# Seven products instead of eight in the first MLP product, and one token part after the other

## The chip, the cores and the metric

The kernel runs on one core of one Trainium2 chip. The metric is device time of one execution, in microseconds, as the median of several runs.

## The reference, cut to what matters

Two blocks follow each other. The first has two layers of mixing (attention and two convolution branches) and an MLP; its layer 0 runs over 512 latent and 256 context tokens, its layer 1 over the 512 latent ones. The second block has two hybrid layers and is not touched. The model width is 1024, the MLP's inner width 4096. What the change bears on, for each layer of the first block:

```python
def sqrelu_mlp(h, w1, w2):
    a = jax.nn.relu(h @ w1)          # h: T x 1024, w1: 1024 x 4096
    return (a * a) @ w2              # w2: 4096 x 1024

h2 = modulate(rmsnorm(xl_new, g_pre_mlp[i]), ml[3], ml[4])
xl_new = xl_new + ml[5] * rmsnorm(sqrelu_mlp(h2, w_mlp_in[i], w_mlp_out[i]), g_post_mlp[i])
```

T is 768 in layer 0 (both kinds of tokens go through the same weights) and 512 in layer 1. Everything is in float32.

## The kernel before, in words

A float32 product is made of three matmuls: every operand is split into a high part (a cast on ScalarE, ACT, line L336) and a low part (a subtraction on VectorE, DVE, L337), and low x high, high x low and high x high are summed in PSUM on TensorE (PE). `mm3` (L368 to L370) does that for one pair of operands; `fm` (L372, its matmul on L383) does it for 128 weight columns over all eight chunks of 128 of the inner dimension. Where there are two token parts (512 and 256 columns in layer 0), `fm` goes through both with each weight part, so that matmuls of 512 and 256 columns alternate.

The MLP (`mlp`, from L1163) works in eight groups of four blocks of 128 columns of W1. For each block: `fm` over T tokens into PSUM, then `square` (relu L1175 and square L1178 on ACT, square and low part L1179 and L1180 on DVE). Then the W2 product of the group for all T/128 token tiles, 512 output columns at a time: 24 matmuls of 512 a tile and group, so 144 in layer 0 and 96 in layer 1, added to the sums in SBUF by DVE (L1220; in group 0 copied by ACT, L1218). The first group is begun while the mixing ends: `early` makes its first two blocks in two parts, and the transposes of the normalized tiles (`prenorm`, L465, with the normalization L460 before and the splits L495 and L496 behind) stand between these parts. Weights come in loads of 512 KB on SyncE's (SP's) queue (L353) into SBUF blocks `at_16_f`, whose places a packer (`pack`) plans ahead; a load's start is set by what freed its place.

The program is written by generators (`yield` gives way to the next stage's work, with a cost in us); a scheduler then sets the order on each engine by the times it expects, and every engine runs its queue in that order. `conv_proj` in layer 0's mixing uses `fm` too, over 512 and 256 columns. In layer 0's MLP the modulation products of layer 1 (L602) and its first columns are woven in.

## Time and profile before

| | us |
| --- | --- |
| median of 3 runs (2879.17 to 2883.06) | 2882.73 |
| the profiled execution's own time | 2879.93 |
| its span | 2878.2 |
| PE busy / DVE busy / ACT busy | 2755.5 / 1623.9 / 1113.5 |

The span runs from the first instruction to the last. An engine is busy while an instruction of it runs; matmuls overlap each other, so that a busy PE says that matmuls follow without a break and not how fast. The time from one matmul's start to the next one's is its pitch. MLP groups run from about 434 to 972 us in layer 0 and from 1281 to 1630 in layer 1.

### The profile page before, as it was taken

The page shows a single profiled execution, that of the slowest core. Times are in us where ns is not written, and L with a number is a line of the kernel's source. Part 1 is how long each engine was busy: PE and PEld are TensorE (multiplying, and loading weights), DVE is VectorE, ACT ScalarE, POOL GpSimd, SP SyncE. Part 2 cuts the span into 40 slices and gives each one's busy share as a digit, 9 for nine tenths or more (in the row PEclk, how much of TensorE's full clock was granted, in tenths as well). Part 3 has the DMA queues.
Part 4 walks back from the last instruction along what each step waited for, and adds up shares of the span by engine and source line. Part 5 has one row for each costly group of instructions (what it writes and reads, how often), then busy time and mean ns, then how long its engine had stood idle before and what let it go on. Part 6 is the DMA issues. An engine that isn't in the chain of part 4 may idle for free. (4 is left out here: it accounts for less than half of the span.)

```text
span 2878.2 us, 37990 instructions
## 1 busy us (share of the span) xinstructions
PE 2755.5 (96%) x14735; PEld 2278.5 (79%) x14735; DVE 1623.9 (56%) x2767; ACT 1113.5 (39%) x2180; POOL 477.6 (17%) x680
## 2 busy tenths in 40 slices
PE   6999999999999899989999899999899999998999
PEld 4877678888888776678888777789788877888887
DVE  4786652434334786653444679655543679565632
ACT  5337643222222526643323444333432543333431
POOL 2024220000000213210000001323221012333111
PEclk9999999999999999999999999999999999999999
DMA  6233444312222333543322422232342522232232
GB/s 225 71 94 112 123 148 145 97 59 63 68 64 68 120 103 96 184 141 108 110 81 80 132 63 69 56 97 62 83 117 75 143 54 57 71 93 63 80 107 81
DMA packets 333564, 277.93 MB, mean 97 GB/s; under 512 B 30340, under 2 KB 275016, under 8 KB 333384
## 3 DMA queue, kind: packets, MB, share of 16 engines
q1 hardware_dynamic: 332410, 273.28, 32.2%
q8 instruction: 116, 1.90, 0.3%
q0 software_dynamic: 704, 2.13, 0.2%
q14 instruction: 64, 0.52, 0.1%
q10 hardware_dynamic: 270, 0.09, 0.0%
HBM read 258.65 MB, written 14.45 MB: 95 GB/s over the span
## 5 line engine op out<-in xcount | busy, mean ns | idle before, releaser
L383 PE MATMUL bank<-at_r,at_r 128*128 128x512 f32 (+1 forms) x5568 | 1214.8, 374 | 2.4 <-ACT at_r L495 2.2
L383 PEld LDWEIGHTS bank<-at_r,at_r 128*128 128x128 f32 x5568 | 965.7, 190 | 187.4 <-issue 8.0
L337 DVE TENSOR_TENSOR at_r<-at_f,at_r 128x1024 fp32r<-128x1024 f32 (+6 forms) x448 | 494.1, 1113 | 486.3 <-ACT at_r L336 380.7
L368 PE MATMUL bank<-at_r,at_r 128*128 128x512 f32 (+5 forms) x1832 | 673.5, 368 | 27.5 <-ACT at_r L336 10.8
L369 PE MATMUL bank<-at_r,at_r 128*128 128x512 f32 (+5 forms) x1832 | 659.6, 360 | 1.8 <-DVE at_r L337 1.8
L370 PE MATMUL bank<-at_r,at_r 128*128 128x512 f32 (+5 forms) x1832 | 658.9, 360 | 0.0
L336 ACT CAST at_r<-at_f 128x1024 fp32r<-128x1024 f32 (+4 forms) x450 | 412.9, 929 | 622.4 <-PE bank L370 190.7
L368 PEld LDWEIGHTS bank<-at_r,at_r 128*128 128x128 f32 x1832 | 350.6, 192 | 104.9 <-issue 16.9
L369 PEld LDWEIGHTS bank<-at_r,at_r 128*128 128x128 f32 x1832 | 351.7, 192 | 49.8 <-DVE at_r L337 4.5
L370 PEld LDWEIGHTS bank<-at_r,at_r 128*128 128x128 f32 x1832 | 350.9, 192 | 48.1 <-issue 1.2
L449 POOL MEMSET at_f<- 128x1 f32 x34 | 3.4, 106 | 888.5 <-DMA at_f<-in_w_q_b_dram 504.6
L1175 ACT ACTIVATE at_f<-bank 128x768 f32<-128x768 f32 (+1 forms) x64 | 45.1, 705 | 258.7 <-PE bank L383 258.7
L516 POOL TENSOR_SCALAR at_f<-at_f,mx 128x768 f32<-128x768 f32 (+3 forms) x112 | 95.3, 853 | 239.8 <-DVE mx L515 221.7
L1220 DVE TENSOR_TENSOR at_f<-at_f,bank 128x512 f32<-128x512 f32 x120 | 81.0, 685 | 54.2 <-PE bank L370 54.0
L1179 DVE TENSOR_TENSOR at_f<-at_f 128x768 f32<-128x768 f32 (+1 forms) x64 | 52.6, 822 | 101.4 <-ACT at_r L1178 101.4
L513 DVE TENSOR_REDUCE mx<-bank 128x1 f32<-128x768 f32 (+1 forms) x80 | 67.6, 845 | 25.7 <-PE bank L370 25.5
L1994 POOL TENSOR_TENSOR at_f<-at_f 128x512 f32<-128x512 f32 x32 | 50.4, 1575 | 178.7 <-DVE at_f L1993 156.5
L336 ACT CAST at_r<-bank 128x256 fp32r<-128x256 f32 (+4 forms) x124 | 51.5, 425 | 68.6 <-PE bank L1943 33.4
L337 DVE TENSOR_TENSOR at_r<-bank,at_r 128x256 fp32r<-128x256 f32 (+4 forms) x124 | 58.9, 483 | 29.7 <-ACT at_r L336 28.7
L514 ACT ACTIVATE at_f<-bank,mx 128x768 f32<-128x768 f32 (+1 forms) x80 | 65.6, 821 | 21.6 <-DVE mx L513 19.0
L1002 PE MATMUL bank<-ident,at_f 128*128 128x128 f32 x416 | 63.0, 279 | 5.6 <-ACT at_f L1006 2.9
L602 PE MATMUL bank<-at_f,at_f 128*32 128x512 f32 x384 | 60.7, 619 | 5.3 <-DMA at_f<-in_w_mod_dram 5.3
(294 smaller groups left out, 2922.7 us busy)
## 6 DMA issues: line engine op xcount, KB each, us to landing
at_f<-in_w_in_dram SPq DMA_DIRECT2D x148, 512.0 KB
at_f<-in_w_mod_dram SPq DMA_DIRECT2D x96, 512.0 KB
at_f<-in_w_mlp_in_dram SPq DMA_DIRECT2D x64, 512.0 KB
at_f<-in_w_mlp_out_dram SPq DMA_DIRECT2D x64, 512.0 KB
at_f<-d SPq DMA_DIRECT2D x28, 512.0 KB
at_f<-in_w_branch_dram SPq DMA_DIRECT2D x48, 256.0 KB
d<-at_f SPq DMA_DIRECT2D x22, 512.0 KB
at_f<-in_w_o_dram SPq DMA_DIRECT2D x16, 512.0 KB
```

What stands on the lines that cost most here:

```text
L336: self.nc.scalar.copy(hi, src)
L337: (self.nc.gpsimd if pool else self.nc.vector).tensor_tensor(lo, src, hi.bitcast(F32), op=OP.subtract)
L368: mm(ps, L[1], R[0], start=start, stop=False)
L369: mm(ps, L[0], R[1], start=False, stop=False)
L370: mm(ps, L[0], R[0], start=False, stop=stop)
L383: mm(ps[:, o:o + b - a], w[x][:, k], hl[y][:, k, a:b], start=k == 0 and j == 0, stop=k == nk - 1 and j == 2)
L513: nc.vector.tensor_reduce(mx[:, 0:1], ps, axis=AX, op=OP.max, negate=True)
L514: nc.scalar.activation(P, ps, AF.Exp, bias=mx[:, 0:1], accum_out=mx[:, 1:2])
L516: nc.gpsimd.tensor_scalar(P, P, mx[:, 2:3], 1.0, op0=OP.mult, op1=OP.mult)
L602: nc.tensor.matmul(ps[q:q + 32], self.sT[:, k], raws[j - 1 + k // 2 % 2][:, k % 2], start=k < 4, stop=k >= 4)
L1002: nc.tensor.transpose(pt[:, k], P[:, k * 128:(k + 1) * 128], self.ident)
L1220: nc.vector.tensor_tensor(y, y, ps[t], op=OP.add)
```

## The change

In groups 1 to 7 of both layers, two blocks of 128 columns of W1 are made together. Tokens, inner dimension and weight columns are each cut in halves, and the 2 x 2 by 2 x 2 product of quarters is made from seven products (`seven`, 84 matmuls of T/2 columns) instead of eight. `wsums` loads 256 columns of W1 (1 MB), makes four sums of weight quarters on DVE and splits all seven weight operands. `hsums` makes four sums of activation quarters once a layer, within the W2 product of group 0: the normalized rows are written to DRAM by `prenorm` (`keep`) and read back, because only their split parts stay in SBUF. Each product is evicted from PSUM by adds on DVE (L1267, one copy on ACT) that combine it with others; relu then works in place in SBUF. `fm` now goes through one token part after the other, and in layer 0 the parts of the MLP's first group are 384 and 384. The packer's constants change too.

```diff
-SPARES, TRIES = (16.0, 8.0, 4.0, 2.0, 1.0, 0.0), 30
+SPARES, TRIES = (4.0, 2.0, 1.0, 0.0), 60
 FLOOR = 60.0
-KEY = lambda B: lambda i: (-min(int((B[i, 4] - B[i, 3]) / 100), 3), -B[i, 0], B[i, 1] - B[i, 2])
+KEY = lambda B: lambda i: B[i, 3] - B[i, 4]
...
     def fm(self, ps, w, parts, nk=8):
         mm = self.nc.tensor.matmul
-        todo, o = [], 0
+        o = 0
         for hl, a, b in parts:
-            todo.append((hl, a, b, o))
+            for k in range(nk):
+                h, q = (hl, k) if len(hl) == 2 else (hl[k // 4 * 2:k // 4 * 2 + 2], k % 4)
+                for j, (x, y) in enumerate(((1, 0), (0, 1), (0, 0))):
+                    mm(ps[:, o:o + b - a], w[x][:, k], h[y][:, q, a:b], start=k == 0 and j == 0,
+                       stop=k == nk - 1 and j == 2)
+                yield 3 * (b - a) / 2400.0
             o += b - a
-        n = sum(b - a for _, a, b, _ in todo)
-        for k in range(nk):
-            for j, (x, y) in enumerate(((1, 0), (0, 1), (0, 0))):
-                for hl, a, b, o in todo:
-                    mm(ps[:, o:o + b - a], w[x][:, k], hl[y][:, k, a:b], start=k == 0 and j == 0,
-                       stop=k == nk - 1 and j == 2)
-            yield 3 * n / 2400.0
...
+            if keep is not None:
+                nc.sync.dma_start(keep.rearrange("p (k f) -> p k f", k=8), y)
...
-        L["h2"], L["h2c"] = self.HL(8, 512), None
+        n = T // 256
+        L["h2"], L["h2c"] = self.HL(8, 128 * n if n > 2 else 512), None
+        L["rows"] = self.dram([T, 1024])
...
+                if T > 512:
+                    L["h2c"] = self.HL(4, 128 * n) + self.HL(4, 128 * n)
...
+    def hsums(self, L):
...
+        B = L["B"] = {x: self.HL(4, 128 * n) for x in names}
+        def one(t):
+            s = slice(t * 128, t * 128 + 128)
+            part = lambda x, src: self.split(src, *(z[:, :, s] for z in B[x]))
+            o, y, d = self.A(8, 128), self.A(8, 128), self.A(2, 4, 128)
+            for z, r in ((o, t), (y, t + n)):
+                nc.sync.dma_start(z, L["rows"][r * 128:(r + 1) * 128].rearrange("p (k f) -> p k f", k=8))
+            sub = lambda z, a, b: nc.vector.tensor_tensor(z, a, b, op=OP.subtract)
+            sub(d[:, 0], y[:, 0:4], o[:, 0:4])
+            sub(d[:, 1], y[:, 4:8], d[:, 0])
+            part("T1", d[:, 0])
+            part("T2", d[:, 1])
+            sub(y[:, 0:4], y[:, 4:8], y[:, 0:4])
+            part("T3", y[:, 0:4])
+            sub(o[:, 4:8], o[:, 4:8], d[:, 1])
+            part("T4", o[:, 4:8])
+            self.F(o, y, d)
...
+    def wsums(self, W, c0):
+        nc = self.nc
+        r = self.raw(8, 256)
+        nc.sync.dma_start(r, W[:, c0:c0 + 256].rearrange("(k p) n -> p k n", p=128))
+        a11, a12, a21, a22 = (r[:, k:k + 4, x:x + 128] for x in (0, 128) for k in (0, 4))
+        s = self.A(2, 4, 128, lead=self.PART)
+        HL = lambda *n: [self.A(*n, dt=F32R, lead=self.PART) for _ in range(2)]
+        tt = nc.vector.tensor_tensor
+        wa, wb, ws = HL(8, 128), HL(4, 128), [HL(2, 4, 128) for _ in range(2)]
+        self.split(r[:, :, 0:128], *wa)
+        tt(s[:, 0], a21, a22, op=OP.add)
+        tt(s[:, 1], s[:, 0], a11, op=OP.subtract)
+        self.split(s, *ws[0])
+        tt(s[:, 0], a11, a21, op=OP.subtract)
+        tt(s[:, 1], a12, s[:, 1], op=OP.subtract)
+        self.split(s, *ws[1])
+        self.split(a22, *wb)
+        self.F(r, s)
...
+    def seven(self, ps, w, h):
+        mm = self.nc.tensor.matmul
+        for k in range(4):
+            for j, (x, y) in enumerate(((1, 0), (0, 1), (0, 0))):
+                mm(ps, w[x][:, k], h[y][:, k], start=k == 0 and j == 0, stop=k == 3 and j == 2)
+            yield 3 * ps.shape[1] / 2400.0
...
+        half, quick = T // 2, True
+        if quick and T > 512:
+            early = later = [(h2, 0, half), (h2c, 0, half)]
...
+        def pair(c0):
+            add = lambda o, a, b: nc.vector.tensor_tensor(o, a, b, op=OP.add)
+            w, held = self.wsums(W1, c0)
+            B, x = L["B"], [self.A(T) for _ in range(2)]
+            u, y = self.A(half), [r[:, i * half:(i + 1) * half] for r in x for i in range(2)]
+            def product(i, j, *sums):
+                ps = self.P(half)
+                yield from self.seven(ps, w[i], B[j])
+                if not sums:
+                    nc.scalar.copy(u, ps)
+                for o, z in sums:
+                    add(o, z, ps)
+                self.F(ps)
+            yield from product("11", "11")
+            yield from product("12", "21", (y[0], u))
+            yield from product("S2", "T2", (u, u))
+            yield from product("S1", "T1", (y[1], u))
+            yield from product("S3", "T3", (y[3], y[1]), (u, u))
+            yield from product("S4", "22", (y[1], y[1]))
+            yield from product("22", "T4", (y[2], u))
+            self.F(u, held)
+            nc.scalar.activation(x[0], x[0], AF.Relu)
+            nc.scalar.activation(x[1], x[1], AF.Relu)
+            for r in x:
+                hi, lo = self.HL(T)
+                nc.scalar.activation(hi, r, AF.Square)
+                nc.vector.tensor_tensor(r, r, r, op=OP.mult)
+                nc.vector.tensor_tensor(lo, r, hi.bitcast(F32), op=OP.subtract)
+                self.F(r)
+                aT.append((hi, lo))
...
+            if quick and g:
+                for p in range(2):
+                    yield from pair((4 * g + 2 * p) * 128)
...
-                ps = self.P(T)
-                yield from self.fm(ps, w, later)
+                ps = self.P(2, 512) if wide else self.P(T)
+                if wide:
+                    for i in range(2):
+                        yield from self.fm(ps[:, i, :half], w, later[i:i + 1])
+                else:
+                    yield from self.fm(ps, w, later)
...
+            if quick and g == 0:
+                sums = self.hsums(L)
...
+                        if sums:
+                            sums.pop(0)()
```

Three places of the new order. On PE, the start of a steady layer-0 group (W2 product of one group, then W1 product of the next), before:

```order
L370 MATMUL bank<-at_16_r,at_12_r 128x512
L383 MATMUL bank<-at_64_r,at_16_r 128x512
L383 MATMUL bank<-at_32_r,at_16_r 128x256
L383 MATMUL bank<-at_64_r,at_16_r 128x512
L383 MATMUL bank<-at_32_r,at_16_r 128x256
L383 MATMUL bank<-at_64_r,at_16_r 128x512
```

and now, the whole W1 product of the group (two pairs of 84):

```order
L370 MATMUL bank<-at_16_r,at_12_r 128x512
L1233 MATMUL bank<-at_24_r,at_16_r 128x384 x17
L1233 MATMUL bank<-at_48_r,at_16_r 128x384 x24
L1233 MATMUL bank<-at_24_r,at_16_r 128x384 x31
L1233 MATMUL bank<-at_24_r,at_8_r 128x384 x12
L1233 MATMUL bank<-at_48_r,at_16_r 128x384 x24
L1233 MATMUL bank<-at_24_r,at_16_r 128x384 x48
L1233 MATMUL bank<-at_24_r,at_8_r 128x384 x12
```

Alternating matmuls of 512 and 256 columns, each with its own weights, have become runs of 384 columns. On DVE, in a steady layer-0 group, before (the adds of the W2 product L1220, the splits of the next weights L337, the squares of a block):

```order
L1220 TENSOR_TENSOR at_16_f<-at_16_f,bank 128x512 x6
L337 TENSOR_TENSOR at_16_r<-at_16_f,at_16_r 128x1024
L1220 TENSOR_TENSOR at_16_f<-at_16_f,bank 128x512 x6
L337 TENSOR_TENSOR at_16_r<-at_16_f,at_16_r 128x1024 x3
L1179 TENSOR_TENSOR at_12_f<-at_12_f 128x768
L1180 TENSOR_TENSOR at_12_r<-at_12_f,at_12_r 128x768
L337 TENSOR_TENSOR at_16_r<-at_16_f,at_16_r 128x1024
L1179 TENSOR_TENSOR at_12_f<-at_12_f 128x768
L1180 TENSOR_TENSOR at_12_r<-at_12_f,at_12_r 128x768
L337 TENSOR_TENSOR at_16_r<-at_16_f,at_16_r 128x1024 x2
L1179 TENSOR_TENSOR at_12_f<-at_12_f 128x768
L1180 TENSOR_TENSOR at_12_r<-at_12_f,at_12_r 128x768
```

and now, from the last adds of the W2 product (L1347) through the weight sums (L1215 to L1219) and splits into the first adds out of PSUM (L1267):

```order
L1347 TENSOR_TENSOR at_16_f<-at_16_f,bank 128x512
L1219 TENSOR_TENSOR at_16_f<-at_32_f,at_16_f 128x512
L1347 TENSOR_TENSOR at_16_f<-at_16_f,bank 128x512
L337 TENSOR_TENSOR at_16_r<-at_16_f,at_16_r 128x1024
L1347 TENSOR_TENSOR at_16_f<-at_16_f,bank 128x512
L337 TENSOR_TENSOR at_16_r<-at_32_f,at_16_r 128x1024
L337 TENSOR_TENSOR at_8_r<-at_32_f,at_8_r 128x512
L1267 TENSOR_TENSOR at_12_f<-at_6_f,bank 128x384
L1267 TENSOR_TENSOR at_6_f<-at_6_f,bank 128x384
L1215 TENSOR_TENSOR at_16_f<-at_32_f 128x512
L1267 TENSOR_TENSOR at_12_f<-at_6_f,bank 128x384
L337 TENSOR_TENSOR at_16_r<-at_32_f,at_16_r 128x1024
```

The weight sums and the adds out of PSUM stand in DVE's one queue between the old work; the low part of the first weight quarter is the split behind the adds of L1347. On PE, at layer 0's entry into the MLP (the last two tiles' transposes, L465 before), before:

```order
L465 MATMUL bank<-ident,at_17_f 128x128 x8
L383 MATMUL bank<-at_64_r,at_16_r 128x512 x25
L465 MATMUL bank<-ident,at_17_f 128x128 x8
L383 MATMUL bank<-at_64_r,at_16_r 128x512 x23
L441 MATMUL bank<-ident,at_2_f 128x103
L441 MATMUL bank<-ident,at_2_f 128x62
L602 MATMUL bank<-at_16_f,at_4_f 32x512 x4
L383 MATMUL bank<-at_32_r,at_16_r 128x256 x48
```

and now:

```order
L464 MATMUL bank<-ident,at_17_f 128x128 x8
L380 MATMUL bank<-at_48_r,at_16_r 128x384 x24
L439 MATMUL bank<-ident,at_2_f 128x103
L439 MATMUL bank<-ident,at_2_f 128x62
L464 MATMUL bank<-ident,at_17_f 128x128 x8
L380 MATMUL bank<-at_48_r,at_16_r 128x384 x24
L380 MATMUL bank<-at_24_r,at_16_r 128x384
L603 MATMUL bank<-at_16_f,at_4_f 32x512
```

Between the two transposes stand 24 matmuls of 384 columns, where 25 of 512 stood.

## Rows read from the trace of the kernel before

**Rows 1.** Page, parts 1 and 2: busy time by engine; PE's granted clock in 40 slices.
```profile
PE 2755.5 (96%) x14735; PEld 2278.5 (79%) x14735; DVE 1623.9 (56%) x2767; ACT 1113.5 (39%) x2180; POOL 477.6 (17%) x680
PEclk9999999999999999999999999999999999999999
```

**Rows 2.** Table of stretches: start:end, length, busy time (instructions) by engine, clock, DMA.
```profile
core 0: us, PE busy (x) PEld busy (x) DVE busy (x) ACT busy (x) POOL busy (x), PEclk, DMA share, GB/s
541.00:608.00 67.00, 67.00 (x342) 56.80 (x341) 25.57 (x32) 15.79 (x17) 0.00 (x0) 1.00 0.24 71
1368.00:1412.00 44.00, 44.00 (x195) 36.43 (x195) 20.44 (x25) 12.80 (x16) 0.00 (x0) 1.00 0.32 96
420.00:434.00 14.00, 12.09 (x64) 9.16 (x63) 7.96 (x16) 6.05 (x11) 0.70 (x1) 0.88 0.77 239
1270.00:1285.00 15.00, 11.39 (x63) 10.40 (x64) 12.21 (x16) 9.95 (x16) 0.55 (x1) 0.66 0.45 149
```

**Rows 3.** Timeline of PE: start, us from first start to last end, line, form, count.
```profile
541.15 0.39 PE L370 MATMUL bank<-at_r,at_r 128*128 128x512 f32 x1
...
547.95 0.39 PE L370 MATMUL bank<-at_r,at_r 128*128 128x512 f32 x1
961.74 0.35 PE L370 MATMUL bank<-at_r,at_r 128*128 128x416 f32 x1
...
964.02 0.35 PE L370 MATMUL bank<-at_r,at_r 128*128 128x416 f32 x1
2255.77 0.31 PE L368 MATMUL bank<-at_r,at_r 128*128 128x332 f32 x1
...
2256.99 0.32 PE L370 MATMUL bank<-at_r,at_r 128*128 128x332 f32 x1
1262.09 6.00 PE L383 MATMUL bank<-at_r,at_r 128*128 128x256 f32 x48
```

**Rows 4.** Timeline of ACT: first and last relu of four, layer 0, layer 1.
```profile
638.86 0.81 ACT L1175 ACTIVATE at_f<-bank 128x768 f32<-128x768 f32 x1 [7.42 <-PE bank L383]
...
664.30 0.81 ACT L1175 ACTIVATE at_f<-bank 128x768 f32<-128x768 f32 x1 [6.79 <-PE bank L383]
1365.52 0.60 ACT L1175 ACTIVATE at_f<-bank 128x512 f32<-128x512 f32 x1 [9.10 <-PE bank L383]
...
1381.84 0.60 ACT L1175 ACTIVATE at_f<-bank 128x512 f32<-128x512 f32 x1 [3.38 <-PE bank L383]
```

**Rows 5.** DVE by line and shape, 541 to 608 us (count | busy us, mean ns); page.
```profile
L337 DVE TENSOR_TENSOR at_r<-at_f,at_r 128x1024 fp32r<-128x1024 f32 x9 | 11.0, 1225 | 24.5 <-ACT at_r L336 24.4
L1220 DVE TENSOR_TENSOR at_f<-at_f,bank 128x512 f32<-128x512 f32 x12 | 8.1, 685 | 3.9 <-PE bank L370 3.8
L1179 DVE TENSOR_TENSOR at_f<-at_f 128x768 f32<-128x768 f32 x4 | 3.8, 957 | 14.5 <-ACT at_r L1178 14.5
L337 DVE TENSOR_TENSOR at_r<-bank,at_r 128x256 fp32r<-128x256 f32 (+4 forms) x124 | 58.9, 483 | 29.7 <-ACT at_r L336 28.7
```

**Rows 6.** ACT by line and shape, 541 to 608 us.
```profile
L336 ACT CAST at_r<-at_f 128x1024 fp32r<-128x1024 f32 x9 | 9.5, 1052 | 33.5 <-PE bank L370 22.1 <-PE bank L383 6.1 <-DMA at_f<-in_w_mlp_out_dram 2.7
```

**Rows 7.** PE's weight loads by line and shape, whole span.
```profile
L383 PEld LDWEIGHTS bank<-at_r,at_r 128*128 128x128 f32 x5568 | 965.7, 190 | 187.4 <-issue 8.0 <-ACT at_r L495 2.6 <-ACT at_r L336 0.8
```

**Rows 8.** Timeline of PE at the entries into the MLP [idle before <-releaser].
```profile
414.57 5.96 PE L383 MATMUL bank<-at_r,at_r 128*128 128x512 f32 x25
422.43 1.09 PE L465 MATMUL bank<-ident,at_f 128*128 128x128 f32 x8 [1.91 <-DVE at_f L460]
423.28 7.09 PE L383 MATMUL bank<-at_r,at_r 128*128 128x512 f32 x23
1271.42 1.97 PE L465 MATMUL bank<-ident,at_f 128*128 128x128 f32 x8 [3.33 <-DVE at_f L460]
1275.58 9.72 PE L383 MATMUL bank<-at_r,at_r 128*128 128x256 f32 x55 [2.19 <-ACT at_r L495]
```

**Rows 9.** Timelines of SP and ACT: a W2 load's issue, and the cast that awaits it.
```profile
687.65 0.37 SPq L353 DMA_DIRECT2D at_f<-in_w_mlp_out_dram  x1
691.05 1.05 ACT L336 CAST at_r<-at_f 128x1024 fp32r<-128x1024 f32 x1 [17.53 <-DMA at_f<-in_w_mlp_out_dram]
```

More of the change, by code (lines that the diff above doesn't have):

```diff
@@ L494, in modulate @@
                 k = slice(ks[h], ks[h] + 4)
-                nc.scalar.copy(hl[0][:, k, s], y[:, h:h + 4])
-                nc.vector.tensor_tensor(hl[1][:, k, s], y[:, h:h + 4], hl[0][:, k, s].bitcast(F32), op=OP.subtract)
+                d = [x[:, k, s] for x in hl] if len(hl) == 2 else [x[:, :, s] for x in hl[k.start // 2:k.start // 2 + 2]]
+                self.split(y[:, h:h + 4], *d)
             self.F(y)
@@ L1161, in post, with end @@
         self.F(j)
+    def hsums(self, L):
+        nc, n = self.nc, L["T"] // 256
+        names = ["T1", "T2", "T3", "T4"]
+        B = L["B"] = {x: self.HL(4, 128 * n) for x in names}
[15 more added lines that the diff above has]
+            self.F(o, y, d)
+        def end():
+            pick = lambda k, a, b: tuple(x[:, k:k + 4, a:b] for x in L["h2"])
+            B["11"], B["21"] = pick(0, 0, 128 * n), pick(4, 0, 128 * n)
+            if n > 2:
+                self.F(L["h2c"][:2])
+                B["22"] = L["h2c"][2:]
+            else:
+                B["22"] = pick(4, 256, 512)
+            L["held"] = [B[x] for x in names] + [L["h2c"][2:] if n > 2 else []]
+        return [lambda t=t: one(t) for t in range(n)] + [end]
@@ new lines, in wsums @@
+    def wsums(self, W, c0):
[16 more added lines that the diff above has]
+        self.F(r, s)
+        pick = lambda p, i: tuple(x[:, i] for x in p)
+        w = {"11": pick(wa, slice(0, 4)), "12": pick(wa, slice(4, 8)), "22": wb, "S1": pick(ws[0], 0),
+             "S2": pick(ws[0], 1), "S3": pick(ws[1], 0), "S4": pick(ws[1], 1)}
+        return w, [wa, wb, ws]
@@ L1184, in mlp @@
         for g in range(NG):
             aT = []
-            up = [self.w_fm(W1, 0, 8, (4 * g + f) * 128) for f in range(2)]
+            if quick and g:
+                for p in range(2):
+                    yield from pair((4 * g + 2 * p) * 128)
+            wide = quick and T > 512
+            up = [] if quick and g else [self.w_fm(W1, 0, 8, (4 * g + f) * 128) for f in range(2)]
             if g == 0:
-                ps = [self.P(T) for _ in up]
-                for hl, a, b in early:
+                ps = [self.P(2, 512) if wide else self.P(T) for _ in up]
+                for i, (hl, a, b) in enumerate(early):
@@ L1191, in mlp @@
                     for w, p in zip(up, ps):
                         o = a if hl is h2 else 512 + a
-                        yield from self.fm(p[:, o:o + b - a], w, [(hl, a, b)])
+                        yield from self.fm(p[:, i, :half] if wide else p[:, o:o + b - a], w, [(hl, a, b)])
                 self.F(up)
@@ L1223, in mlp @@
             else:
-                self.F(h2, h2c if h2c else [])
+                self.F(h2, L["held"] if quick else h2c if h2c else [])
                 ready()
```

15 lines of the change are left out of this document (9 added, 6 removed).

## The prediction

> **What bounds the kernel now.** I read the page first: TensorE (PE) is busy 2755.5 of 2878.2 us, VectorE (DVE) 1623.9, ScalarE (ACT) 1113.5, and PE's granted clock stands at 9 tenths or more in every slice [rows 1]. An average can hide stages with other limits, so I went on to the table by stretches, for one steady group of four blocks in the MLP of either layer: PE is busy 67.00 of 67.00 us in layer 0 and 44.00 of 44.00 in layer 1, DVE only 25.57 and 20.44, ACT 15.79 and 12.80, at a granted clock of 1.00 [rows 2]. So in the stage that the change touches the end is set by how many matmuls PE issues and at what pitch, and DVE has more than half its time to give away.
>
> PE's busy time counts overlapping instructions (a matmul lasts 0.39 us and the next starts 0.23 later), so I cost matmuls by their **pitch**, start to start [rows 3]. 512 columns: (547.95 - 541.15) / 30 = 0.227 us. 416 columns: (964.02 - 961.74) / 12 = 0.190. 332 columns: (2256.99 - 2255.77) / 8 = 0.1525. 256 columns: 48 matmuls take 6.00 us from the first start to the last end. The line through 332 and 416 columns has 0.446 ns a column, that through 332 and 512 has 0.414; by the second, 256 columns come to 0.121. That fits: 47 x 0.121 = 5.69, which leaves 0.31 for the last one's own length. I take 0.120. For 384 columns the two lines give 0.174 to 0.176. So a matmul costs about 13 ns and 0.418 ns a column; small ones lose little.
>
> **What the change takes away on PE.** One block of 128 weight columns is 24 matmuls (8 chunks of K, three each) of 512, and in layer 0 24 more of 256 between them. The relu at its end starts every (664.30 - 638.86) / 3 = 8.48 us in layer 0 and (1381.84 - 1365.52) / 3 = 5.44 in layer 1 [rows 4]; by pitches layer 1 is 24 x 0.227 = 5.45, so the two views agree.
> - Layer 0, a pair of blocks: 2 x 8.48 = 16.96 before. After: 7 products x 4 chunks x 3 = 84 matmuls of 384 columns, 84 x 0.174 = 14.62 (14.78 at 0.176). Gain 2.34. Seven groups of two pairs: 14 x 2.34 = 32.8.
> - Layer 1: 10.88 before, 84 x 0.120 = 10.08 after. Gain 0.80, x 14 = 11.2. Here seven eighths would be 9.52; the 13 ns of twice as many matmuls eat 0.6 of the 1.36.
> - Group 0 of layer 0 now runs 48 matmuls of 384 a block: 8.35 for 8.48, x 4 = 0.5.
> - The conv projection of layer 0 (10 blocks through the same helper): 512 columns for all of K and then 256, 24 x (0.227 + 0.120) = 8.33 for 8.48, x 10 = 1.5.
>
> Together **46 us**, all on the engine that sets the end.
>
> **What it adds on DVE and ACT, and whether PE waits for it.** A split of 1024 is 1.05 us on ACT and 1.225 on DVE [rows 5, 6]. A DVE operation on 512 columns with an operand in PSUM is 0.685. No row has 384 or 256 columns with an SBUF output added from PSUM; the nearest is the 256-column split out of PSUM at 0.483 [rows 5], so I take 0.56 for 384 and bound it by 0.48 and 0.685, and 0.42 for 256, bounded by 0.34 (half of 0.685) and 0.483. A pair in layer 0 then costs DVE 4 sums (4 x 0.69) + 3 splits of 1024 and one of 512 (3 x 1.225 + 0.69) + 7 adds of 384 (3.9) + the squares as before (4 x 0.957 = 3.8, [rows 5]) = 14.9, against 6.3 before (two splits and the squares). In layer 1: 2.8 + 4.4 + 2.9 + 4 x 0.69 = 12.8, against 5.2. With the adds and splits of the W2 product, which stay (13.1 in layer 0, 12 x 0.685 + 4 x 1.225; 10.4 in layer 1, 8 and 4 of them), DVE has 43 of 62 us of a layer-0 group and **36 of 42 us of a layer-1 group**. ACT rises by some 2 us a pair and stays under half. So in bulk the cover holds, though thinly in layer 1; the question is order, since DVE runs its queue in order. I walked the new order with these durations. In layer 1 every add is done before its bank is wanted again, and the weight splits come ahead of their first matmul. In layer 0 the first matmuls of a group wait for the low part of the first weight quarter, whose split stands behind the add of the last W2 tile: 0.3 us a group, x 7 = 2. If the cover failed in layer 1 it would show as a wait of the length of one add or split a pair (0.4 to 1.2 us), up to 17 us in 14 pairs; I charge it to the range.
>
> The weights come as one load of 1 MB a pair instead of two of 512 KB. A 512 KB load landed 691.05 - 687.65 = 3.4 us after its issue [rows 9]; for 1 MB I take between that and twice it, 6.8, and 2.3 us for the first split. The order leaves some 14 to 17 us of PE work between the matmul that frees the buffer and the first one that uses the new weights (before: 33 to 90), so the load is hidden with 5 us in hand. SP's queue has only such loads there; what queues behind a late one is the next W2 weights.
>
> **Where a stretch gets worse.** Three, none priced by a row of its own.
> - Into the MLP of layer 0. Today 25 matmuls of 512 (5.96 us) stand between the last two transposes, PE then waits 1.91 us for the DVE operation at L460, and the next 23 run in 7.09 us, where 23 x 0.227 = 5.2 [rows 8]; the clock in that stretch is 0.88 [rows 2]. Now 24 of 384 (4.2 us) stand there, so that wait grows by 1.8; the last half tile's split stands one place further back on DVE, 0.7 more; and the clock may be low for longer, about 1. SP gets a row write ahead of every store of the residual, which waits for that tile's normalized rows with the next W1 loads behind it; these have tens of us in hand. The worst row of this kind is layer 1's entry: waits of 3.33 and 2.19 us and a clock of 0.66 over 15 us [rows 2, 8], which cost 5.5 of idle time and some 3 of slow matmuls (55 in 9.72 us, 6.6 at 0.120); I take +3.5, bounds 0 and +9.
> - Group 0 of layer 0. Writing the rows (6 x 512 KB) and reading them back, then 4 differences and 4 splits of 512 for each of three tile pairs (3 x 4 x (0.69 + 0.69) = 16.6 us of DVE) lie inside a W2 product of 32.7 us. DVE waits there for the read-back with W2 adds behind it, and PE waits for their banks: one load's 3.4 us, or one set of sums (5.5) late: +5, bounds 0 and +12.
> - Group 0 of layer 1: two tile pairs, less in the queue: +2, bounds 0 and +6.
>
> Memory is planned afresh, so loads in the second block start at other times; PE's order there is nearly the one before. 0, +-5.
>
> **Sum.** 2879.9 (the profiled execution's own time; its span of 2878.2 and 1.7 around it) - 46 + 2 + 3.5 + 5 + 2 = 2846.4. The profiled execution lies 2.8 under the median of the runs, so **2849** for the median.
>
> The Trainium skill has a rule that would turn this: "TensorE: Matmul & The Clock Gate", section "Back-to-back issue gap", says that in a stream of weight loads and matmuls the spacing is set by both, with about 81 ns at 128 columns and 131 ns at 512. An estimate on that line (98 ns at 256, 114 at 384) makes a layer-1 pair dearer (8.2 us for 6.3) and a layer-0 pair cheaper (9.6 for 10.9), nearly no change in all. The trace disagrees: 227 ns at 512 and at most 125 at 256 [rows 3], nearly proportional to columns. It is the first rival that carries what is left of it.
>
> **Rivals.**
> - *Weight loads pace the small matmuls* (slower). Each matmul here has its own weight load, 190 ns on average [rows 7]. If it were not hidden behind the matmul before, 84 x 0.190 = 15.96 a pair: layer 1 +5.08 x 14 = +71, layer 0 -1.00 x 14 = -14, with the conv and group-0 terms +18: 2882.7 + 75 = 2958. It decides from a pitch of 130 ns at 256 columns (10.88 / 84) in layer 1. Against it: 48 such matmuls in 6.00 us, each with a load.
> - *DVE sets the pace in order* (same or slower). The gain is 46 over 28 pairs, 1.64 us a pair; a wait of that size in each, about one split and one add, cancels it. If an add waits behind a split that itself waits for a load (1.225 + 0.685 + a late load's 2), 3.9 a pair gives 2882.7 + 28 x (3.9 - 1.64) = 2946. For it: 86% of a layer-1 group. Against it: the walk finds 0 to 0.3 a group. At half that wait it is 2880, no change.
> - *The entries and group 0 cost their upper bounds, or layer 1 waits a little* (gain smaller): 9 + 12 + 6 + 2, and up to 8 in layer 1, leave 9 to 17: 2866 to 2874.
> - *Everything is covered*: 2882.7 - 46 = 2837, less with kinder loads: 2832.
>
> **How the numbers follow.** Forecast (2838 to 2860) 0.58; all covered (2831 to 2838) 0.14; smaller gain (2860 to 2876) 0.16; DVE in order 0.09, of which 0.05 within 0.2% and 0.04 slower; loads 0.03, of which 0.02 slower and 0.01 within. Faster 0.88, same 0.06, slower 0.06; 0.2% (5.8 us) is about what a measurement of this kernel can tell from none. The range takes in the forecast, all but the edge of the full cover, and the lower two thirds of the smaller gain: 2832 to 2870.
>
> **What would show it.** The relus of a layer-0 group should come with 14.6 us between pairs, W2 stretch unchanged at 32.7, so a group's period falls from 66.6 to about 62.0 (now 2 x 16.96 + 144 x 0.227), in layer 1 from 43.6 to 42.0. Matmuls of the new line should start 0.174 and 0.120 apart. DVE should be busy about 43 and 36 us a group, with PE idle under 0.5. The entry of layer 0 should show a longer wait on the normalization and a clock under 0.9; group 0 a few waits of PE on W2 adds. I am wrong if the pitch of 256 columns is over 125 ns, if PE waits for DVE in every pair, or if the second block's stretch moves by more than 5 us.

## The result, and the profile after

| | before | after |
| --- | --- | --- |
| median, us (four runs of each on one chip) | 2881.42 | 2849.89 (2842.43 to 2860.24) |
| ratio, 95% interval | | 0.9899 (0.9880 to 0.9918) |
| the profiled execution / its span | 2879.93 / 2878.2 | 2854.19 / 2852.5 |
| predicted median | | 2849 (2832 to 2870) |

The kernel became 31.5 us faster. The forecast was right in sign and size; two places that its sum had priced at nothing moved by 16 and by 9 us in opposite directions, as is shown below.

The page of the kernel after answers to [rows 1]: PE is 30 us less busy, DVE 217 us more, and still far from full.

```profile
PE 2725.1 (96%) x15071; PEld 2302.0 (81%) x15071; DVE 1841.3 (65%) x3171; ACT 1184.3 (42%) x2284; POOL 484.4 (17%) x680
PEclk9999999999999999999999999999999999999999
```

The table of stretches, for one steady group of each layer and for the entry of layer 0, answers to [rows 2] (start:end, length, busy time and instructions by engine, clock, DMA share, GB/s):

```profile
660.00:722.00 62.00, 62.00 (x314) 56.23 (x313) 40.11 (x55) 18.98 (x22) 0.00 (x0) 1.00 0.22 68
1373.00:1415.00 42.00, 42.00 (x266) 38.24 (x265) 33.56 (x51) 16.29 (x22) 0.00 (x0) 1.00 0.33 101
420.00:434.00 14.00, 10.84 (x46) 9.45 (x47) 9.34 (x18) 7.22 (x13) 0.55 (x1) 0.76 0.88 292
```

The stretch of a steady group's period is now 62 us long and not 67, 42 and not 44, and PE is idle in neither, at a granted clock of 1.00. DVE is busy 40 of 62 and 34 of 42 us (forecast: 43 and 36). PE's timeline gives the period and the pitches; columns as in [rows 3]:

```profile
639.77 20.27 PE L1233 MATMUL bank<-at_r,at_r 128*128 128x384 f32 x116
...
721.80 0.39 PE L368 MATMUL bank<-at_r,at_r 128*128 128x512 f32 x1
...
783.71 0.39 PE L368 MATMUL bank<-at_r,at_r 128*128 128x512 f32 x1
...
1402.73 4.84 PE L1233 MATMUL bank<-at_r,at_r 128*128 128x256 f32 x39
1407.41 4.48 PE L1233 MATMUL bank<-at_r 128*128 128x256 f32 x36
1411.73 3.04 PE L1233 MATMUL bank<-at_r,at_r 128*128 128x256 f32 x24
...
1456.55 0.40 PE L368 MATMUL bank<-at_r,at_r 128*128 128x512 f32 x1
...
1498.49 0.40 PE L368 MATMUL bank<-at_r,at_r 128*128 128x512 f32 x1
```

The first matmul of a W2 product comes every 783.71 - 721.80 = **61.9 us** in layer 0 and 1498.49 - 1456.55 = **41.9** in layer 1. The pitch of 384 columns is (20.27 - 0.3) / 115 = 0.174 us, that of 256 columns (1407.41 - 1402.73) / 39 = 0.120 and (1411.73 - 1407.41) / 36 = 0.120. All four are the forecast's numbers. The new adds out of PSUM take 550 ns on 384 columns and 417 on 256 (forecast 0.56 and 0.42 us); by line and shape, over the same two stretches:

```profile
L1267 DVE TENSOR_TENSOR at_f<-at_f,bank 128x384 f32<-128x384 f32 x14 | 7.5, 550 | 2.9 <-PE bank L1233 2.7
L1267 DVE TENSOR_TENSOR at_f<-at_f,bank 128x256 f32<-128x256 f32 x15 | 6.0, 417 | 2.5 <-PE bank L1233 2.4
```

**Where the time went.** I laid the two traces side by side: for the same PE instruction (the first of a W2 product, where there is one), its start after minus its start before.

| place in the program | start before, us | after minus before | share of the place |
| --- | --- | --- | --- |
| before the MLP of layer 0 | 402.8 | 0.0 | 0 |
| first W2 product of layer 0 | 455.6 | +4.0 | entry and W1 product of group 0: +4.0 |
| W2 product of group 1 | 529.2 | +5.0 | +1.0, in which 4.7 were gained |
| of group 2 | 597.5 | +0.3 | -4.7 |
| of group 6 | 863.8 | -18.1 | -18.4, four groups of 4.6 |
| behind layer 0's exit | 1032.7 | -6.3 | **+11.8**, in which 4.6 were gained |
| first W2 product of layer 1 | 1294.4 | -5.8 | +0.5 |
| last W2 product of layer 1 | 1599 | -16.9 | -11.1, seven groups of 1.6 |
| end of the span | 2878.2 | -25.7 | **-8.8** |

So the steady groups gave what the sum said, and three places away from them moved: the first 130 us of layer 0's MLP cost 4.0 + 0.5 + 1.0 + 4.7 = 10.2 us (what a place gained in its own products is added back), layer 0's exit cost 11.8 + 4.6 = 16.4, and the second block gave 8.8.

The exit is read from the timeline of all engines, from 909 us on, where PE ends the last product of the last group (columns: start, duration, engine, line, operation; in brackets the idle time before, and what ended it):

```profile
908.75 0.84 ACT L1290 ACTIVATE at_f<-at_f 128x768 f32<-128x768 f32 x1
909.17 1.16 DVE L337 TENSOR_TENSOR at_r<-at_f,at_r 128x832 fp32r<-128x832 f32 x1
...
910.26 1.04 DVE L1295 TENSOR_TENSOR at_r<-at_f,at_r 128x768 fp32r<-128x768 f32 x1
...
911.22 1.05 DVE L337 TENSOR_TENSOR at_r<-at_f,at_r 128x832 fp32r<-128x832 f32 x1
...
912.20 0.96 DVE L1294 TENSOR_TENSOR at_f<-at_f 128x768 f32<-128x768 f32 x1
913.08 1.02 DVE L337 TENSOR_TENSOR at_r<-at_f,at_r 128x832 fp32r<-128x832 f32 x1
914.02 0.96 DVE L1295 TENSOR_TENSOR at_r<-at_f,at_r 128x768 fp32r<-128x768 f32 x1
914.13 1.04 ACT L336 CAST at_r<-at_f 128x1024 fp32r<-128x1024 f32 x1 [3.03 <-DVE at_r L337]
...
915.23 1.22 PE L368 MATMUL bank<-at_r,at_r 128*128 128x512 f32 x2 [7.43 <-ACT at_r L336]
```

PE stands 7.43 us at the first matmul of the last W2 product. It waits for the cast of that product's weights (914.13), the cast for a split on DVE that ended at 914.1. That split (128x832, L337) makes weights of layer 1's mixing, and three such splits stand in DVE's queue between the squares (L1294, L1295) of the last pair. The cast reads nothing that this split writes. What it can wait for is its place in SBUF, if the unsplit form of those weights held it until then; the trace shows no addresses, and the run with earlier places below tests it. Before, there was no idle time of PE here. The stretch from the last product's end to the point where the offset settles (1026.4 us after, 1032.7 before) holds the same PE work. The first row is the wait itself, the second the whole stretch after the change, the third the stretch before:

```profile
910.00:920.00 10.00, 4.73 (x10) 3.28 (x11) 7.55 (x9) 4.24 (x5) 5.05 (x6) 0.50 0.00 0
...
907.50:1026.40 118.90, 95.28 (x448) 79.76 (x447) 81.88 (x148) 59.85 (x139) 25.29 (x52) 0.89 0.39 109
```

```profile
930.00:1032.70 102.70, 92.40 (x450) 79.65 (x449) 71.98 (x138) 54.32 (x132) 19.50 (x46) 0.93 0.43 121
```

118.9 us for 102.7, with 448 and 450 matmuls. PE is idle 23.6 us where it was 10.3: 7.4 more by the one wait, 5.9 by longer waits between the normalizations, transposes and products of layer 1's start. The other 2.9 are matmuls at a lower granted clock, above all those right behind the wait, at 0.50.

From the end of layer 1's MLP on, PE has the same work in both (1205.5 and 1205.8 us busy), with 48.5 us idle where 59.2 stood; 2 of these 10.7 us were lost just ahead of the stretch (after, then before):

```profile
1598.00:2852.00 1254.00, 1205.49 (x6591) 1027.95 (x6591) 769.66 (x1467) 481.21 (x1040) 281.49 (x373) 0.99 0.30 84
```

```profile
1613.00:2878.00 1265.00, 1205.84 (x6593) 1026.41 (x6593) 772.20 (x1467) 481.26 (x1041) 281.99 (x373) 0.99 0.30 83
```

### The profile page after: what moved, and what is told of

Its sections match the earlier page's. It is cut to its first block, busy times and chain, and to the rows that moved or that the text cites. A ratio compares the mean times of both kernels' runs of the same rounds, so it can differ in the third digit from the quotient of the medians.

```text
span 2852.5 us, 39343 instructions
## 1 busy us (share of the span) xinstructions
PE 2725.1 (96%) x15071; PEld 2302.0 (81%) x15071; DVE 1841.3 (65%) x3171; ACT 1184.3 (42%) x2284; POOL 484.4 (17%) x680
## 5 line engine op out<-in xcount | busy, mean ns | idle before, releaser
L380 PE MATMUL bank<-at_r,at_r 128*128 128x512 f32 (+2 forms) x3552 | 821.9, 385 | 1.6 <-ACT at_r L336 1.4
L336 ACT CAST at_r<-at_f 128x1024 fp32r<-128x1024 f32 (+5 forms) x586 | 506.8, 879 | 719.5 <-DMA at_f<-in_w_mlp_in_dram 108.3
L337 DVE TENSOR_TENSOR at_r<-at_f,at_r 128x1024 fp32r<-128x1024 f32 (+6 forms) x584 | 609.1, 1054 | 261.4 <-ACT at_r L336 221.1
L380 PEld LDWEIGHTS bank<-at_r,at_r 128*128 128x128 f32 x3552 | 639.8, 191 | 122.2 <-issue 7.7
L368 PEld LDWEIGHTS bank<-at_r,at_r 128*128 128x128 f32 x1832 | 349.9, 191 | 106.4 <-ACT at_r L336 19.5
L369 PEld LDWEIGHTS bank<-at_r,at_r 128*128 128x128 f32 x1832 | 350.7, 191 | 52.4 <-DVE at_r L337 5.3
L370 PEld LDWEIGHTS bank<-at_r,at_r 128*128 128x128 f32 x1832 | 350.2, 191 | 46.9
L1233 PE MATMUL bank<-at_r,at_r 128*128 128x384 f32 (+1 forms) x1848 | 290.7, 316 | 1.6 <-DVE at_r L337 1.5
L1233 PEld LDWEIGHTS bank<-at_r,at_r 128*128 128x128 f32 x1848 | 286.5, 189 | 5.6 <-ACT at_r L336 2.1
L1267 DVE TENSOR_TENSOR at_f<-at_f,bank 128x384 f32<-128x384 f32 (+1 forms) x196 | 91.9, 484 | 47.9 <-PE bank L1233 46.4
L1347 DVE TENSOR_TENSOR at_f<-at_f,bank 128x512 f32<-128x512 f32 x120 | 80.4, 683 | 21.4 <-PE bank L370 21.0
L337 DVE TENSOR_TENSOR at_r<-bank,at_r 128x256 fp32r<-128x256 f32 (+4 forms) x124 | 59.0, 484 | 48.9 <-ACT at_r L336 47.8
L603 PE MATMUL bank<-at_f,at_f 128*32 128x512 f32 x384 | 68.2, 610 | 7.1 <-DMA at_f<-in_w_mod_dram 7.1
```

The costliest lines, as they stand in the source:

```text
L336: self.nc.scalar.copy(hi, src)
L337: (self.nc.gpsimd if pool else self.nc.vector).tensor_tensor(lo, src, hi.bitcast(F32), op=OP.subtract)
L368: mm(ps, L[1], R[0], start=start, stop=False)
L369: mm(ps, L[0], R[1], start=False, stop=False)
L370: mm(ps, L[0], R[0], start=False, stop=stop)
L380: mm(ps[:, o:o + b - a], w[x][:, k], h[y][:, q, a:b], start=k == 0 and j == 0, stop=k == nk - 1 and j == 2)
```

## The experiments

Twelve kernels ran, on three chips, each beside the kernel before on the same chip (2874.58, 2875.52 and 2874.76 us there). All ratios are to it, with their 95% interval. "Offset" is meant as in the table above, and the cost of a place is taken as there.

**The kernel after, unchanged**, to know what a trace of it repeats.

> The changed kernel once more, for a second trace: its four runs lay 18 us apart (2842.4 to 2860.2), those of before 4. Theory (PE's issue sets the end, and the gain is the sum of the pitches less waits at the MLP's entry and exit): ratio 0.988 to 0.991, and against the first trace the steady groups keep their periods of 61.9 and 41.9 us within 0.2; what differs between the two traces lies where PE waits. Rival (DVE's queue sets the pace in the pairs): the groups themselves differ from trace to trace by over 1 us.

2842.28 us, 0.9886 (0.9869 to 0.9902). Against its first trace this one is 4 us earlier by 373 us, then 4.9 to 5.1 earlier through every group of layer 0 from 501 to 955 (PE waits 7.43 us in the same place), 10.4 earlier through all groups of layer 1, and 13.9 at the end. By the table's reckoning its exit costs 14.1 us, where the first trace has 16.4, and its second block gives 12.3 for 8.8. The difference between executions comes in steps of 1 to 3 us in the mixing and the second block. So a difference of 0.3 us a group can be read from single traces, and one of under 5 us outside the groups can't.

**Only one layer.** What does each layer give alone? (The line that decides; the edit also writes the rows for the one layer only and keeps layer 0's parts of 384 in both.)

```diff
-        half, quick = T // 2, True
+        half, quick = T // 2, T > 512      # the other run: T <= 512
```

> Seven products in layer 0 only; layer 1 as before. Theory (PE's issue): layer 1's periods return from 41.9 to 43.5 us, so 11 us are given back: about 2861. Rival (DVE in order paces layer 1, where it is busy 36 of 42 us): layer 1 has little to give back, 2850 to 2853.

> Seven products in layer 1 only; layer 0 with eight, its tokens in two parts of 384 one after the other, no rows written for it. Theory (PE's issue): before less 11 in layer 1, less 4 for 384 + 384 instead of 512 and 256 in turns and 1.5 in the conv projection, and layer 0's entry without the added wait: about 2865. Rival (the gain is made in the steady groups of layer 0 alone and the rest is the plan): 2875 to 2882.

Layer 0 alone: 2852.25, 0.9918 (0.9903 to 0.9933). This lies in the rival's range, but that range was written on the scale of the first chip. Against the unchanged kernel after on the same chip (2842.28) it is 10.0 us slower, and in the traces it loses 1.6 us a group in layer 1, and 9.9 by the end: layer 1's term. Layer 1 alone: 2852.44, 0.9918 (0.9903 to 0.9933), much better than expected. Its groups of layer 1 give what they should (-0.5 to -11.2 us against before); the exit of layer 0 costs 5.8 and not 16.4, and the second block runs 15.8 us shorter (-11.2 to -27.0) though nothing in it was edited. The two alone give 22 us each and together 32: the groups add up, the places between them don't. Its groups of layer 0 have eight products of 384 columns, one part after the other; they run 0.58 us a group shorter (+1.6 to -1.3 in five), which is the forecast's 0.5 for group 0.

**The packer's constants**, on either kernel.

```diff
-SPARES, TRIES = (4.0, 2.0, 1.0, 0.0), 60
+SPARES, TRIES = (16.0, 8.0, 4.0, 2.0, 1.0, 0.0), 30
 FLOOR = 60.0
-KEY = lambda B: lambda i: B[i, 3] - B[i, 4]
+KEY = lambda B: lambda i: (-min(int((B[i, 4] - B[i, 3]) / 100), 3), -B[i, 0], B[i, 1] - B[i, 2])
```

> The changed kernel with the packer's constants of before. In the first trace of the changed kernel PE waits 7.4 us after layer 0's last pair for the cast of the first W2 weights, loses some 9 more by the start of layer 1, and gains 9 in the second block. Rival (these three come from the memory plan): the 7.4 goes or moves and the second block's offset against before falls from -9 to about 0, so 2840 to 2862, steady periods the same. Theory without the plan (they come from the products themselves): all three stay, 2850.

> The kernel before with the packer's three changed constants and nothing else. The changed kernel with the constants of before came out level with before (ratio 1.0005), and kernels with the new constants are 10 to 17 us faster in the second block, which the products don't touch. Plan theory: the constants alone bring the second block's part, so 2857 to 2866 on the scale of 2874.6 (ratio 0.994 to 0.997). Rival (the constants only let the seven products keep their gain, and the second block moved with the new blocks' sizes): ratio 1.000, within 0.998 to 1.002.

The kernel after with the old constants: 2875.90, **1.0005** (0.9995 to 1.0014), the whole gain gone. The kernel before with the new ones (the diff reversed): 2873.02, 0.9990 (0.9976 to 1.0005), nothing. The first lies outside both ranges of its expectation; the second is what the rival gave. With the old constants the steady groups have a period of 62.0, and the 7.4 us wait at the exit is not there (the exit costs 7.9). The trace ends 24 us behind the first trace of the kernel after and 38 behind the second; 21 of it arise in 470 to 566 us, behind group 0. PE's, SP's and DVE's timelines with the old constants:

```profile
493.10 1.22 PE L368 MATMUL bank<-at_r,at_r 128*128 128x512 f32 x2 [3.88 <-ACT at_r L336]
...
521.96 4.21 PE L1233 MATMUL bank<-at_r,at_r 128*128 128x384 f32 x15 [9.71 <-DVE at_r L337]
```

```profile
494.33 9.87 SPq L1180 DMA_DIRECT2D at_f<-d  x2
511.60 0.38 SPq L590 DMA_DIRECT2D at_f<-in_w_mod_dram  x1
512.16 0.38 SPq L1208 DMA_DIRECT2D at_f<-in_w_mlp_in_dram  x1
```

```profile
507.03 2.02 DVE L1181 TENSOR_TENSOR at_f<-at_f 128x512 f32<-128x512 f32 x3 [2.16 <-DMA at_f<-d]
...
519.35 0.69 DVE L1215 TENSOR_TENSOR at_f<-at_f 128x512 f32<-128x512 f32 x1 [6.24 <-DMA at_f<-in_w_mlp_in_dram]
```

And SP's in the kernel after:

```profile
488.33 0.81 SPq L1180 DMA_DIRECT2D at_f<-d  x2
490.58 0.38 SPq L1208 DMA_DIRECT2D at_f<-in_w_mlp_in_dram  x1
```

The two read-backs of the last tile pair (L1180) take 9.87 us from the first issue to the end of the second, and 0.81 in the kernel after. A modulation load (L590) behind them goes out only at 511.60. The first 1 MB of W1 (L1208) stands behind both in SP's queue and is issued at 512 and not 491, its sums start when it has landed at 519, and PE stands 9.71 us in front of the first of the seven products. Only the packer's constants differ, so the loss comes from the plan of memory, and the constants belong to this change: seven products with the old plan give nothing.

In the second block the constants alone gain 2.7 us, the products with the old constants some 4 to 5, and both together 8.8 and 12.3 in the two traces; the constants by themselves do not explain it.

**`fm` alone, one part after the other** (in the kernel before).

```diff
         for hl, a, b in parts:
-            todo.append((hl, a, b, o))
...
-                for hl, a, b, o in todo:
+            for k in range(nk):
+                for j, (x, y) in enumerate(((1, 0), (0, 1), (0, 0))):
                     mm(ps[:, o:o + b - a], w[x][:, k], hl[y][:, k, a:b], start=k == 0 and j == 0,
...
```

> The kernel before with only the helper's order changed: one token part after the other, 512 columns for all of K and then 256. Theory (pitches): 0.227 + 0.120 against 0.354, 24 of them a block, 42 blocks in layer 0: 7 us less, ratio 0.9976, a steady layer-0 group 66.0 instead of 66.6. Rival (in turns or one after the other is the same for PE, since every matmul has its own weight load): 66.6, ratio 1.000.

2887.39, 1.0048 (1.0031 to 1.0065): slower, where a gain was expected. The gain in the groups is there: a layer-0 group has 66.0 us for 66.6, and the offset is -6.2 by 969 us. The conv projection's 1.5 can't be read: the offset is -1.3 behind it (184 us), +1.5 at 196 and -0.3 at 402.8. The exit of layer 0 then takes the gain back with two waits (3.2 and 0.5 us there before), and the second block loses 8 us more. PE's timeline at this exit:

```profile
994.02 0.48 PE L722 MATMUL bank<-ident,at_f 128*128 128x128 f32 x1 [6.40 <-ACT at_f L703]
...
1018.75 0.47 PE L722 MATMUL bank<-ident,at_f 128*128 128x128 f32 x1 [5.42 <-DVE at_f L704]
```

So an edit that shortens PE's work, with nothing added anywhere, cost 12 us in the medians (7 in the trace), and in the trace all of the loss lies in stages that it doesn't touch.

**Is DVE's cover thick?** The kernel after without the four weight sums of a pair, and with four more.

```diff
-        tt(s[:, 0], a21, a22, op=OP.add)
-        tt(s[:, 1], s[:, 0], a11, op=OP.subtract)
-        self.split(s, *ws[0])
...
+        for x in ws:
+            self.split(r[:, :, 128:256].rearrange("p (i k) n -> p i k n", i=2), *x)
```

> The changed kernel without the four weight sums of a pair on DVE (the splits that followed them take raw weight columns instead, so the output is not the reference's): DVE has 2.76 us less a pair, 77 us in all, PE's matmuls and the memory plan are the same. Theory (DVE is covered in the pairs): steady periods stay 61.9 and 41.9 us, and the time moves by under 5 us, at the entries and layer 0's exit only. Rival (DVE in order holds up each pair): up to 1.4 us a pair comes back, 20 to 40 us.

```diff
+        tt(s[:, 0], a21, a22, op=OP.add)
+        tt(s[:, 1], s[:, 0], a21, op=OP.subtract)
...
+        tt(s[:, 0], a11, a21, op=OP.subtract)
+        tt(s[:, 0], a11, a21, op=OP.subtract)
```

> The changed kernel with four more additions of 512 on DVE in every pair, which write values that are overwritten: 2.76 us a pair, so DVE is busy about 48 of 62 us in a layer-0 group and 41.5 of 42 in a layer-1 group; PE and the memory plan are the same. Theory (DVE is covered while it has room): layer 0's period stays 61.9 within 0.5 us, layer 1's rises by 0 to 2 us a group, and the time by 0 to 15. Rival (DVE in order holds up each pair already): each pair pays the 2.76 us, both periods rise by 5.5, the time by 77.

Without sums: 2853.99, 0.9927 (0.9912 to 0.9942). The steady groups don't change: the same stretches are full of PE, with 4.5 to 4.8 us less on DVE.

```profile
660.00:722.00 62.00, 62.00 (x314) 56.18 (x314) 35.63 (x47) 18.93 (x23) 0.00 (x0) 1.00 0.21 69
1373.00:1415.00 42.00, 42.00 (x267) 38.25 (x266) 28.73 (x43) 16.91 (x22) 0.00 (x0) 1.00 0.33 101
```

With four more (5.5 us of DVE a group): 2876.35, 1.0007 (0.9995 to 1.0018). Layer 0's period grows by 0.35 us to 62.3. Layer 1's grows by 1.1: its seven groups take 301.6 us (1311.21 to 1612.82, first W2 product to last) for 293.7 (1288.65 to 1582.37), and PE waits five times for DVE's splits and squares, which it never does in that stretch of the kernel after. The trace ends 26.7 us behind the first of the kernel after; 21 of it arise at 434 to 592 again. The stretch of a group and a half in layer 0, the relus 62.27 us apart, PE's waits for DVE in layer 1 (us in total, times, longest), and PE's wait behind group 0:

```profile
600.00:700.00 100.00, 99.86 (x502) 90.15 (x501) 74.16 (x101) 33.31 (x39) 0.00 (x0) 1.00 0.22 69
```

```profile
662.92 0.84 ACT L1293 ACTIVATE at_f<-at_f 128x768 f32<-128x768 f32 x1
...
725.19 0.84 ACT L1293 ACTIVATE at_f<-at_f 128x768 f32<-128x768 f32 x1
```

```profile
PE bank L1237 <- DVE at_r L337: 3.9, 3, 1.9
PE bank L368 <- DVE at_r L1299: 0.8, 2, 0.5
```

```profile
513.39 2.93 PE L1237 MATMUL bank<-at_r,at_r 128*128 128x384 f32 x8 [8.57 <-DVE at_r L337]
```

So DVE is covered in the groups as they stand: 5 us less a group gain nothing. The cover is thick in layer 0, where 5.5 us more cost 0.35, and thin in layer 1, where they cost 1.1. Between the MLP's start (402.8) and 592 us, five of the nine edited versions of the kernel after lose 10 to 19 us against its first trace, most of it behind group 0, with less work on DVE as with more. Layer 0's exit goes with DVE's load: it costs 8.8 us without the sums and 19.9 with four more, for 16.4 and 14.1 as it is. Order and places there may have moved too, so this is a sign and no proof that DVE's queue sets it.

**The way through DRAM.** No rows are written; the sums read rows of W2 instead.

```diff
-..., keep=L["rows"][t * 128:(t + 1) * 128])
+..., keep=None)
-                nc.sync.dma_start(z, L["rows"][r * 128:(r + 1) * 128].rearrange("p (k f) -> p k f", k=8))
+                nc.sync.dma_start(z, self.i["w_mlp_out"][L["i"]][r * 128:(r + 1) * 128].rearrange("p (k f) -> p k f", k=8))
```

> The changed kernel without writing the normalized rows to DRAM; the activation sums are made from rows of W2 instead, loads that wait for nothing written before (so the output is not the reference's). Sums, splits and load sizes are the same. Against before, the changed kernel gives back 5.5 us between 400 and 600 us (entry into the MLP and group 0). Theory (the path through DRAM is hidden but for a wait or two): 0 to 4 us come back, all before 600 us, ratio 0.987 to 0.989. Rival (write and read-back are what the entry pays): 5 us or more come back.

2846.17, 0.9894 (0.9875 to 0.9913), no better than the kernel after (0.9886 and 0.9899). Between 402.8 us and the W2 product of group 2 (597.5, on the clock of before) its offset goes from -0.4 to -1.2, in the two traces of the kernel after from 0.0 to +0.3 and from -4.0 to -4.7: 0.1 to 1.1 us come back. So writing the rows and waiting for them costs nothing that can be told from the scatter; what the rest of the 10 us there consists of is not shown.

**The exit.** Three attempts to take its wait away: the planner keeps the places of the last W2 weights free earlier (its "leads"); with that, the four splits of layer 1's first weights go to GpSimd (POOL); or the splits alone.

```diff
+                self.RAW, self.PART = 40.0, 32.0
                 wu = [[self.w_tm(W2, 4 * g + 2 * u, h * 512, 512) for u in range(2)] for h in range(2)]
+                self.RAW, self.PART = 16.0, 8.0
```

```diff
-                    nxt["lead"] = [self.parts(r) for r in self.lead_raw(nxt, range(4))]
+                    nxt["lead"] = [self.parts(r, pool=True) for r in self.lead_raw(nxt, range(4))]
```

> The changed kernel, with the planner told to keep the places of the last group's W2 weights free 40 and 32 us ahead instead of 16 and 8. In the trace PE waits 7.4 us after layer 0's last pair because the cast of the first W2 weights goes to a place that a split of layer 1's weights reads last, late in DVE's queue. Place theory: the 7.4 us go, ratio to before about 0.986, unless the next wait stands close behind. Rival (the DVE queue is simply full there and the cast's own split or the last squares come just as late): PE waits on for 5 us or more, 0.988 to 0.989.

> The changed kernel with two edits at layer 0's exit: the W2 places kept free earlier as in the run before, and the four splits of layer 1's first weights (1.02 us each on DVE) made on GpSimd, which has been idle there for 475 us. In the trace of the run with the places alone PE still waits 4.7 us for W2 splits that stand behind those four in DVE's queue. Queue theory: the wait shrinks by 3 to 5 us and layer 1 starts 5 to 10 us earlier, ratio 0.984 to 0.987. Rival (the exit is bound by the chain of normalizations between the layers, whatever is on DVE): the offset at layer 1's start stays, 0.988 to 0.991.

> The changed kernel with the four splits on GpSimd alone, places as in the change. The first W2 cast waits for the last of these splits to leave its place; GpSimd takes about 2 us for each, so it comes later if they run one after the other (8 us against 4). Queue theory: the wait of 7.4 us stays or grows, while what stands behind it on DVE shrinks by 4: ratio 0.986 to 0.990. Rival (the splits on DVE are all there is to it): the wait of 7.4 falls by 3 to 5 us, 0.984 to 0.987.

Leads alone: 2850.51, 0.9915 (0.9899 to 0.9931). The 7.4 us wait is gone, and 40 us later nothing is left of it: against the second trace of the unchanged kernel after, the offset goes from +4.7 to -3.0 at the W2 product and back to +6.0 at 956 us, and the exit costs 16.5. PE's timeline, and DVE's behind it:

```profile
913.82 0.96 PE L368 MATMUL bank<-at_r,at_r 128*128 128x512 f32 x3 [2.24 <-ACT at_r L336]
...
917.20 0.79 PE L369 MATMUL bank<-at_r,at_r 128*128 128x512 f32 x1 [2.42 <-DVE at_r L337]
```

```profile
911.09 2.10 DVE L337 TENSOR_TENSOR at_r<-at_f,at_r 128x832 fp32r<-128x832 f32 x2
913.11 1.04 DVE L1294 TENSOR_TENSOR at_f<-at_f 128x768 f32<-128x768 f32 x1
914.07 1.05 DVE L337 TENSOR_TENSOR at_r<-at_f,at_r 128x832 fp32r<-128x832 f32 x1
915.04 0.95 DVE L1295 TENSOR_TENSOR at_r<-at_f,at_r 128x768 fp32r<-128x768 f32 x1
915.92 1.22 DVE L337 TENSOR_TENSOR at_r<-at_f,at_r 128x1024 fp32r<-128x1024 f32 x1
```

The low part of the W2 weights (128x1024) now stands behind the same 832 splits and squares, so the wait for a place became a wait for DVE's queue. Leads and GpSimd together: 2849.44, 0.9907 (0.9890 to 0.9925). A split takes 2.0 to 3.0 us on GpSimd and DVE is free of it; PE waits 2.09 us at the W2 product, and the exit costs 7.5 us for 16.4 and 14.1 in the unchanged kernel after:

```profile
L337 POOL TENSOR_TENSOR at_r<-at_f,at_r x4: 1985/2018/2979, 912.9 to 933.2; 128x832 fp32r<-128x832 f32 x4
```

```profile
929.04 1.34 PE L368 MATMUL bank<-at_r,at_r 128*128 128x512 f32 x3 [2.09 <-DVE at_r L1295]
```

But it had lost 15 us by 592 against the kernel after (waits of 4.41 at the entry, 4.58 and 5.28 behind group 0). GpSimd alone: 2850.48, 0.9906 (0.9886 to 0.9927); a wait of 8.2 us stays, so both edits were needed to take it away, though the exit costs 10.6 here. No version beats the kernel after.

Taken together, the expectations were right about the steady groups and mostly wrong about the total: of the times or ratios that their theories gave, only the unchanged kernel's came out, and two more (without rows, GpSimd alone) were missed by under 0.1%. What they left out lies in the places between the groups.

## Why the prediction was right, point by point

- **PE's gain in the groups**, 32.8 and 11.2 us. Right: 4.6 to 4.7 us a group in layer 0 and 1.6 in layer 1, from pitches read off a line through other column counts. This term carries the result, and single-layer runs confirm it apart.
- **Weight loads pace the small matmuls** (the first rival). Not so: 0.120 us at 256 columns, under the 0.130 from which it would have decided. The rule of the Trainium skill ("TensorE: Matmul & The Clock Gate", section "Back-to-back issue gap") disagrees with this trace again: an estimate on its line gives 98 and 114 ns at 256 and 384 columns, where 120 and 174 were measured.
- **DVE in order**. Right: 40 and 34 us a group against 43 and 36, and PE idle 0.0 in the stretches. Here the forecast's 2 us of waits (0.3 a group) did not come at all or are under 0.1 a group (61.9 and 41.9 against 61.9 and 42.0 by pitches alone). That the cover is thin in layer 1 was right too: 5.5 us more on DVE cost 1.1 a group there and 0.35 in layer 0.
- **Conv, 1.5, and group 0, 0.5**. The edit of `fm` alone shows the 0.6 a group (66.0 for 66.6, with 512 columns and then 256), and layer 1 alone shows it with 384 and 384. The conv term is not shown: at 402.8 us the offset is -0.3 with `fm` alone, 0.0 in the first trace after and -4.0 in the second, so that it is lost in the scatter of the mixing.
- **Entry of layer 0 and group 0**, +3.5 and +5. Right in sum and in place: 4.5 and 5.7 (the table's +4.0 and +1.0, plus the 0.5 and 4.7 gained there). A count that leaves group 1's gain out gives 5.5 for both; 10.2 is right. The entry looks as told: the stretch 420:434 has a granted clock of 0.76 for 0.88 and 3.2 us of idle PE for 1.9 [rows 2]. But its ends were too near: five edited versions of the kernel after cost 10 to 19 us more there.
- **Group 0 of layer 1**, +2: about 0.
- **The exit of layer 0**. The step that failed: it has no term. I priced the entries, where the edit's own instructions stand, and gave what comes behind the last group to "memory planned afresh, 0, +-5", and that for the second block alone. It cost 16.4 (14.1 in the second trace). That the last pair's adds, squares and weight splits are more work on DVE, in a place where the next layer's splits stand too, could have been looked up in the order. The trace shows 7.4 of the 16.4 as one wait, behind such a split; with the old constants of the packer that wait is gone and the exit costs 7.9, so about half of it goes with the plan of memory.
- **The second block**, 0 +-5: -8.8, outside the bounds, and -21 to +8 in kernels that touch nothing in it. I had said that I'd be wrong if it moved by more than 5, and in that step I was.

By terms: -32.4 (layer 0's groups) - 0.5 + 10.2 (entry and group 0) + 16.4 (exit) + 0.5 - 11.1 (layer 1, its group 0 included) - 8.8 = -25.7 us for the profiled pair, where the forecast had -33.5 (2879.9 to 2846.4). The miss of 7.8 is the exit's 16.4 less the second block's 8.8, and small terms that cancel. The median came closer than that, within 1 us of 2849, by chance: the profiled execution of before lies 1.5 us under the median of its four runs (2.8 under that of the three that the forecast had), and that of after 4.3 over.

What stays open is why the second block gained: PE waits some 10 us less there, with the same work; neither the constants alone nor the products with the old constants gain as much, and no run changed one thing in it alone. And what is left of the exit once its wait and DVE's queue are relieved, 7.5 of the 16 us, was not taken apart.
